# Low parts, squares and a norm's step move between GpSimd, adding DMAs and VectorE in a decoder trunk

## The chip, the cores and the metric

The kernel runs on one core of a Trainium2 chip. The metric is the device time of one execution in microseconds; the time before is the median of three runs. The engines are named as the profile names them: PE (TensorE matmuls), PEld (its weight loads), DVE (VectorE), ACT (ScalarE), POOL (GpSimd) and SP (SyncE, which here only issues DMAs). Each engine works through its own queue in order.

## The reference, cut to what matters

A decoder trunk of two layers, T = 512 rows, D = 1024. Layer 0 mixes tokens by differential attention with 8 heads, layer 1 by retention with 4 heads; behind each comes an MLP with a squared ReLU and a gated embedding.

```python
def sq_relu_mlp(xn, w1, w2):
    h = jax.nn.relu(xn @ w1)          # 1024 -> 4096
    return (h * h) @ w2               # 4096 -> 1024

def diff_attention(xn, ...):
    ...
    attn = a[:, :, 0] - lam * a[:, :, 1]
    o = attn @ v
    o = rms_norm(o, g_sub) * (1.0 - lambda_init)     # per head: the sub-norm
    return o @ w_o

def reference(x, p, ...):
    for i in range(2):
        h = rms_norm(x, norm_mix[i])
        x = x + (diff_attention(h, ...) if i % 2 == 0 else retention(h, ...))
        x = x + sq_relu_mlp(rms_norm(x, norm_mlp[i]), mlp_w1[i], mlp_w2[i])
        gate = jax.nn.sigmoid(rms_norm(x, norm_pe[i]) @ pe_w_gate[i])
        x = x + gate * (p[i] @ pe_w_up[i])
    return x
```

All is float32.

## The kernel before

Activations lie transposed, as 8 tiles of 128 features x 512 rows. Every factor of a matmul is kept as a pair: a high part (rounded to the matmul's format by a cast) and a low part (the value minus the high part). `mm3` (L262 to L266) forms one product as three matmuls, high x high (L264), high x low (L265) and low x high (L266).

**Weights.** The class `Weights` streams the weights in the order of their use, four pairs ahead of the one that PE reads. `load` fetches a 512 KB tile `raw` (three buffers, fetched by SP in program order), ACT casts it to `wh` (L101), and DVE writes `wl` = raw - wh (L105); there are five buffers each for `wh` and `wl`. While `W.by_dma` is set, the low part is made otherwise: ACT writes `wl` = -raw, rounded (L93), and POOL issues a DMA that adds `raw` onto `wl` in flight (L94). A raw buffer is free again when its last reader has finished, here that DMA. `by_dma` is set at the start of the attention (L408) and cleared in the MLP of layer 0, chunk 0, at hidden unit 4 (L754).

**The MLP.** It runs in four chunks of 1024 hidden features. In each chunk eight hidden units fill a PSUM tile `ph`; DVE drains it with the ReLU and the norm's factor into `ht` (L768), ACT squares it (L772), and `hh`, `hl` are split off by ACT (L241) and DVE (L242). The second matrix of the first three chunks (`MIXED`) goes by a Strassen scheme of seven products instead of eight. A chunk has two such rounds, r = 0 and r = 1. The scheme needs differences of the hidden blocks, `hu` (L786 to L788, split at L242), and sums and differences of the weight blocks, built by `Weights.mixed` on DVE: s1 = a21 + a22 (L129), s2 = s1 - a11 (L132), s4 = a12 - s2 (L136) and s3 = a11 - a21 (L139). The products run in the order a11, s1, s2, s4, s3, a12, a22. For each, ACT casts the high part (L146), and DVE subtracts it for the low part (L154), but for a11 and a22, where ACT writes the negative high part (L149) and POOL issues a DMA that fetches the block from HBM once more and adds it (L150).

`mix_round` (L710) accumulates the products in PSUM tiles called `py`, then layer, chunk, round, bank and half: py101b is layer 1, chunk 0, round 1, bank b, half 1. Bank b has three buffers, banks c and a two each. A finished part is added to the residual `x` by DVE (L729), and this frees the bank for the next round.

**The other places.** `squares` (L308) adds up squares of rows for a norm; ACT squares, and POOL adds (L314) unless another engine is given. In the attention each head ends in `values` (L562), which squares the head's PSUM tile `po` on ACT and splits the square into `osq...h` and `osq...l`, the low part on POOL, and in `sub_norm` (L575), whose steps go over ACT, DVE (L584), POOL (L585) and DVE (L586, which reads `po` last and frees its bank, and L587). The attention's units are set by a plan written by hand (`place`). At the end of the retention eight tiles `pus` of the last embedding are computed, copied from PSUM by ACT (L1030) and parked in HBM by DMAs from ACT's queue (L1031).

Apart from the hand plan and the DMAs kept in program order, the framework's scheduler sets the order of the instructions on each engine. It can put an instruction elsewhere when the work around it changes.

Of the kernel before, what the change touches and what calls it, by code (L numbers as in the profile page):

```python
# [13 lines left out]
ALU = mybir.AluOpType  # L14
AX = mybir.AxisListType

P = 128
# [47 lines left out]
class Weights:  # L65
# [42 lines left out]
    def mixed(self, kind, w, first):  # L108

        nc, mix = self.nc, self.mix  # L110
        i = len(self.made)
# [34 lines left out]
        nc.scalar.copy(out=hi, in_=t)  # L146
        if kind in ("a11", "a22"):

            nc.scalar.activation(out=lo, in_=hi.bitcast(F32), func=AF.Copy, scale=-1.0)  # L149
            nc.gpsimd.dma_start(  # L150
                out=lo.rearrange("p (j n) -> p j n", j=2), in_=source(0 if kind == "a11" else 3), accum_op=ALU.add
            )
        else:
            nc.vector.tensor_tensor(out=lo, in0=t, in1=hi.bitcast(F32), op=ALU.subtract)  # L154
# [13 lines left out]
def decoder_trunk(ctx: ExitStack, tc, xT, pT, small, dist, decay, ident,  # L168
# [200 lines left out]
    for k in range(KD):  # L369
        t = slot(f"xin{k}")  # L370
        load(t, xT[k])
        z.append(make_z(t, C_MIX, k))
        if k % 2 == 0:
            W.load()
            W.parts = 1
        squares(acc, t, k)

# [10 lines left out]
    with tc.tile_pool(name="at", bufs=1) as ap:  # L388
# [41 lines left out]
        gs = ap.tile([P, 1], F32, name="gs")  # L430
        nc.vector.tensor_scalar(out=gs, in0=sm[:, C_GSUB : C_GSUB + 1], scalar1=1.0 - LAM_INIT, scalar2=None, op0=ALU.mult)

# [129 lines left out]
        def values(h, kt):  # L562
# [7 lines left out]
            if kt == NT - 1:  # L570
                sq = slot("osq")
                nc.scalar.activation(out=sq, in_=po[h], func=AF.Square)
                po[h] = po[h], sq, slots(f"osq{h}", sq, lo_engine=nc.gpsimd)

        def sub_norm(h):  # L575
# [8 lines left out]
            nc.vector.scalar_tensor_tensor(out=u, in0=pn, scalar=P * EPS, in1=u, op0=ALU.add, op1=ALU.mult)  # L584
            nc.gpsimd.tensor_scalar(out=u, in0=u, scalar1=-0.5 / P, scalar2=1.5, op0=ALU.mult, op1=ALU.add)  # L585
            nc.vector.scalar_tensor_tensor(out=sq, in0=ps, scalar=gs, in1=sq, op0=ALU.mult, op1=ALU.mult)  # L586
            nc.vector.tensor_tensor(out=sq, in0=sq, in1=u, op=ALU.mult)  # L587
            oT[h] = slots(f"oT{h}", sq)
# [114 lines left out]
    def mlp(z, acc, layer, late_at=2):  # L703
# [43 lines left out]
        with tc.tile_pool(name=f"mlp{layer}", bufs=1) as mp:  # L747
            W.sums = mp
            for c in range(4):
# [3 lines left out]
                def begin(i):  # L753
                    if (layer, c, i) == (0, 0, 4):  # L754
                        W.by_dma = False
# [125 lines left out]
    with tc.tile_pool(name="zp", bufs=1) as zp:  # L881
# [9 lines left out]
        with tc.tile_pool(name="ret", bufs=1) as ap:  # L891
# [134 lines left out]
            for m in range(KD):  # L1026
# [3 lines left out]
                nc.scalar.copy(out=t, in_=pu)  # L1030
                nc.scalar.dma_start(out=up1[m // 2][:, m % 2, :], in_=t)  # L1031
            acc = project(RH - 1, go_before)
# [87 lines left out]
```

## Time and profile before

| | |
|---|---|
| Median of 3 runs | 1477.12 us (1475.58 to 1477.51) |
| Profiled execution, its own time | 1478.01 us |
| Its span in the trace | 1476.2 us |
| PE busy | 1444.1 us, 98% |
| DVE busy | 931.1 us, 63% |
| ACT busy | 728.0 us, 49% |
| POOL busy | 184.5 us, 12% |
| Mean granted clock of PE | 0.997 |

The execution is a little longer than its span in the trace, since some of it lies around the traced instructions. PE is the engine that is busy nearly all the time, so the list of its waits is short, and the other engines' timelines tell what each wait came from. A wait is put down to the instruction or DMA that came last; a DMA's time is that from its issue to its landing.

### The profile page before, as it was taken

The page shows a single profiled execution, that of the slowest core. Times are in us where ns is not written, and L with a number is a line of the kernel's source. Part 1 is how long each engine was busy: PE and PEld are TensorE (multiplying, and loading weights), DVE is VectorE, ACT ScalarE, POOL GpSimd, SP SyncE. Part 2 cuts the span into 40 slices and gives each one's busy share as a digit, 9 for nine tenths or more (in the row PEclk, how much of TensorE's full clock was granted, in tenths as well). Part 3 has the DMA queues.
Part 4 walks back from the last instruction along what each step waited for, and adds up shares of the span by engine and source line. Part 5 has one row for each costly group of instructions (what it writes and reads, how often), then busy time and mean ns, then how long its engine had stood idle before and what let it go on. Part 6 is the DMA issues. An engine that isn't in the chain of part 4 may idle for free.

```text
span 1476.2 us, 19408 instructions
## 1 busy us (share of the span) xinstructions
PE 1444.1 (98%) x7532; PEld 1224.4 (83%) x7532; DVE 931.1 (63%) x1465; ACT 728.0 (49%) x1091; POOL 184.5 (12%) x151
## 2 busy tenths in 40 slices
PE   9999989999999999999999999999999999999998
PEld 7777767889898988888888888888779889898887
DVE  6766777676676764486364555544698576675445
ACT  6777777754444444354442432433565354443432
POOL 4112112100000000211120210301230000000020
PEclk9999999999999999999999999999999999999999
DMA  6644566856355452243223232132334637445332
GB/s 227 143 115 114 129 168 142 216 143 184 104 136 151 113 165 93 63 165 122 79 83 105 65 112 93 58 128 72 129 100 113 173 86 186 114 121 152 98 114 86
DMA packets 65132, 183.14 MB, mean 124 GB/s; under 512 B 6033, under 2 KB 6545, under 8 KB 65041
## 3 DMA queue, kind: packets, MB, share of 16 engines
q1 hardware_dynamic: 51888, 147.31, 30.7%
q0 software_dynamic: 11424, 30.41, 12.0%
q10 hardware_dynamic: 1728, 4.20, 0.8%
q8 instruction: 59, 0.97, 0.3%
q14 instruction: 33, 0.26, 0.1%
HBM read 157.77 MB, written 6.29 MB: 111 GB/s over the span
## 4 chain that ended last, share of the span: by engine, by line
PE 77%; DMA 9%; DVE 5%; ACT 4%; issue 4%; POOL 1%; SPq 0%; DVEq 0%; POOLq 0%; ACTq 0%
PE ph L265 7%; PE ph L264 7%; PE ph L266 7%; DMA raw<-in_w 6%; PE pg L264 2%; PE pg L266 2%; PE pg L265 2%; PE rv L265 2%; PE py L265 2%; PE rqk L265 2%; PE rv L266 2%; PE rqk L266 2%; PE py L266 2%; PE py L264 2%; PE rv L264 2%
## 5 line engine op out<-in xcount | busy, mean ns | idle before, releaser
L101 ACT CAST wh<-raw 128x1024 fp32r<-128x1024 f32 (+1 forms) x163 | 170.2, 1046 | 345.2 <-PE ph L265 85.9
L105 DVE TENSOR_TENSOR wl<-raw,wh 128x1024 fp32r<-128x1024 f32 (+1 forms) x163 | 208.1, 1278 | 62.3 <-ACT wh L101 61.3
L265 PE MATMUL ph<-zl,wh 128*128 128x512 f32 x512 | 199.5, 390 | 0.0
L264 PE MATMUL ph<-zh,wh 128*128 128x512 f32 x512 | 199.3, 389 | 0.0
L266 PE MATMUL ph<-zh,wl 128*128 128x512 f32 x512 | 199.2, 389 | 0.0
L265 PEld LDWEIGHTS ph<-zl,wh 128*128 128x128 f32 x512 | 96.1, 188 | 20.6 <-DVE zl L245 0.8
L266 PEld LDWEIGHTS ph<-zh,wl 128*128 128x128 f32 x512 | 96.1, 188 | 19.9
L264 PEld LDWEIGHTS ph<-zh,wh 128*128 128x128 f32 x512 | 96.1, 188 | 19.8
L768 DVE SCALAR_TENSOR_TENSOR ht<-ph,rsm 128x512 f32<-128x512 f32 x64 | 43.9, 688 | 98.8 <-PE ph L266 98.6
L150 POOL DMA_DIRECT2D wl<-in_w x24 | 29.0, 1281 | 440.5 <-ACT wl L149 375.9
L146 ACT CAST wh<-mix 128x1024 fp32r<-128x1024 f32 x36 | 37.9, 1053 | 86.0 <-PE ph L265 23.3
L146 ACT CAST wh<-raw 128x1024 fp32r<-128x1024 f32 x48 | 49.2, 1049 | 56.3 <-PE ph L265 23.0
L265 PE MATMUL pqk<-wl,zh 128*128 128x512 f32 x128 | 51.1, 399 | 1.2 <-DMA wl<-raw 1.2
L264 PE MATMUL pqk<-wh,zh 128*128 128x512 f32 x128 | 51.6, 403 | 0.0
L264 PE MATMUL pg<-zh,wh 128*128 128x512 f32 (+1 forms) x136 | 51.2, 377 | 0.0
L266 PE MATMUL pg<-zh,wl 128*128 128x512 f32 (+1 forms) x136 | 51.2, 377 | 0.0
L265 PE MATMUL pg<-zl,wh 128*128 128x512 f32 (+1 forms) x136 | 51.2, 376 | 0.0
L266 PE MATMUL pqk<-wh,zl 128*128 128x512 f32 x128 | 51.0, 398 | 0.0
L264 PE MATMUL rg<-zh,wh 128*128 128x512 f32 x128 | 50.2, 392 | 0.0
L265 PE MATMUL rg<-zl,wh 128*128 128x512 f32 x128 | 50.1, 391 | 0.0
L266 PE MATMUL rg<-zh,wl 128*128 128x512 f32 x128 | 50.0, 390 | 0.0
L265 PE MATMUL rv<-wl,zh 128*128 128x512 f32 x128 | 49.8, 389 | 0.0
(1136 smaller groups left out, 4049.2 us busy)
## 6 DMA issues: line engine op xcount, KB each, us to landing
raw<-in_w SPq DMA_DIRECT2D x140, 512.0 KB, 3.8
wl<-raw POOLq DMA_DIRECT2D x34, 512.0 KB, 5.3
wl<-in_w POOLq DMA_DIRECT2D x24, 512.0 KB, 8.1
raw<-in_w_qk SPq DMA_DIRECT2D x16, 512.0 KB, 3.7
raw<-in_w_g SPq DMA_DIRECT2D x16, 512.0 KB, 3.8
raw<-in_w_rv SPq DMA_DIRECT2D x16, 512.0 KB, 3.6
raw<-in_w_rqk SPq DMA_DIRECT2D x16, 512.0 KB, 4.5
raw<-in_w_rg SPq DMA_DIRECT2D x16, 512.0 KB, 3.6
```

The source lines that it names most:

```text
L101: nc.scalar.copy(out=hi[:, s], in_=raw[:, s])
L105: e.tensor_tensor(out=lo[:, r], in0=raw[:, r], in1=hi[:, r].bitcast(F32), op=ALU.subtract)
L146: nc.scalar.copy(out=hi, in_=t)
L150: nc.gpsimd.dma_start(out=lo.rearrange("p (j n) -> p j n", j=2), in_=source(0 if kind == "a11" else 3), accum_op=ALU.add)
L264: nc.tensor.matmul(ps, a[0], b[0], start=start, stop=False, skip_group_check=on)
L265: nc.tensor.matmul(ps, a[0], b[1], start=False, stop=False, skip_group_check=on)
L266: nc.tensor.matmul(ps, a[1], b[0], start=False, stop=stop, skip_group_check=on)
L768: nc.vector.scalar_tensor_tensor(out=half, in0=s[1].rearrange("p (a n) -> p a n", a=2), scalar=0.0, in1=rs.rearrange("p (a n) -> p a n", a ...
```

## The change

Six edits, each of which takes work from POOL or from ACT's queue:

- `mixed`: only a22 gets its low part by an adding DMA; a11's is now made by DVE at L154. This concerns 12 products (2 layers, 3 chunks, 2 rounds).
- `by_dma` is cleared at hidden unit 0 in place of 4, so four more weights, the last of layer 0's first hidden units, get `wl` from DVE at L105.
- The first `squares` of the kernel: its seven adds go from POOL to DVE.
- `values`: the low parts of the eight heads' squares go from POOL to DVE.
- `sub_norm`: POOL's step goes. The constants are folded into `gs`, and two fused DVE operations take the place of POOL's and the two DVE operations behind it. The one that reads `po` is now the last.
- The eight DMAs of `pus` are issued by POOL in place of ACT.

```diff
--- before.py
+++ after.py
@@ -144,11 +144,11 @@
         hi = self.pool.tile([P, 1024], F32R, name=f"wh{i}", tag="wh", bufs=W_BUFS)
         lo = self.pool.tile([P, 1024], F32R, name=f"wl{i}", tag="wl", bufs=W_BUFS)
         nc.scalar.copy(out=hi, in_=t)
-        if kind in ("a11", "a22"):
+        if kind == "a22":
 
             nc.scalar.activation(out=lo, in_=hi.bitcast(F32), func=AF.Copy, scale=-1.0)
             nc.gpsimd.dma_start(
-                out=lo.rearrange("p (j n) -> p j n", j=2), in_=source(0 if kind == "a11" else 3), accum_op=ALU.add
+                out=lo.rearrange("p (j n) -> p j n", j=2), in_=source(3), accum_op=ALU.add
             )
         else:
             nc.vector.tensor_tensor(out=lo, in0=t, in1=hi.bitcast(F32), op=ALU.subtract)
@@ -373,7 +373,7 @@
         if k % 2 == 0:
             W.load()
             W.parts = 1
-        squares(acc, t, k)
+        squares(acc, t, k, nc.vector)
 
     def up_unit(pu, wu, p, m):
         for j in range(2):
@@ -428,7 +428,7 @@
         nc.vector.tensor_scalar(out=gq, in0=sm[:, C_GQ : C_GQ + 1], scalar1=-(DH ** -0.5), scalar2=None, op0=ALU.mult)
         gk = sm[:, C_GK : C_GK + 1]
         gs = ap.tile([P, 1], F32, name="gs")
-        nc.vector.tensor_scalar(out=gs, in0=sm[:, C_GSUB : C_GSUB + 1], scalar1=1.0 - LAM_INIT, scalar2=None, op0=ALU.mult)
+        nc.vector.tensor_scalar(out=gs, in0=sm[:, C_GSUB : C_GSUB + 1], scalar1=-(1.0 - LAM_INIT) / (2.0 * P), scalar2=None, op0=ALU.mult)
 
         for tt in range(NT):
             put_v(pv[tt], 0, tt)
@@ -570,7 +570,7 @@
             if kt == NT - 1:
                 sq = slot("osq")
                 nc.scalar.activation(out=sq, in_=po[h], func=AF.Square)
-                po[h] = po[h], sq, slots(f"osq{h}", sq, lo_engine=nc.gpsimd)
+                po[h] = po[h], sq, slots(f"osq{h}", sq)
 
         def sub_norm(h):
             ps, sq, pair = po.pop(h)
@@ -582,9 +582,8 @@
             u = slot("osu")
             nc.scalar.activation(out=u, in_=sq, func=AF.Square)
             nc.vector.scalar_tensor_tensor(out=u, in0=pn, scalar=P * EPS, in1=u, op0=ALU.add, op1=ALU.mult)
-            nc.gpsimd.tensor_scalar(out=u, in0=u, scalar1=-0.5 / P, scalar2=1.5, op0=ALU.mult, op1=ALU.add)
-            nc.vector.scalar_tensor_tensor(out=sq, in0=ps, scalar=gs, in1=sq, op0=ALU.mult, op1=ALU.mult)
-            nc.vector.tensor_tensor(out=sq, in0=sq, in1=u, op=ALU.mult)
+            nc.vector.scalar_tensor_tensor(out=u, in0=u, scalar=-3.0 * P, in1=sq, op0=ALU.add, op1=ALU.mult)
+            nc.vector.scalar_tensor_tensor(out=sq, in0=ps, scalar=gs, in1=u, op0=ALU.mult, op1=ALU.mult)
             oT[h] = slots(f"oT{h}", sq)
 
 
@@ -751,7 +750,7 @@
                 hs, st = [], {}
 
                 def begin(i):
-                    if (layer, c, i) == (0, 0, 4):
+                    if (layer, c, i) == (0, 0, 0):
                         W.by_dma = False
                     return W.next(), ps_mm(f"ph{layer}{c}{i}")
 
@@ -1028,7 +1027,7 @@
                 up_unit(pu, wu, p1, m)
                 t = zslot(f"pus{m}", F32)
                 nc.scalar.copy(out=t, in_=pu)
-                nc.scalar.dma_start(out=up1[m // 2][:, m % 2, :], in_=t)
+                nc.gpsimd.dma_start(out=up1[m // 2][:, m % 2, :], in_=t)
             acc = project(RH - 1, go_before)
             z = zn
 
```

The matmuls are the same, 7517 in the program. POOL has 156 instructions before and 125 after, ACT 1041 and 1017, DVE 1467 and 1498. Behind L584 the lines after are one lower than before, so L729 is L728, L768 is L767, and L786 is L785. Three places show what stands in a row.

DVE at the start of the second round in layer 1, chunk 1, before (numbers behind a name tell buffers apart; py110b and py110c are banks of round 0, L129 and L132 build s1 and s2, and raw_0 is a11):

```order
L729 TENSOR_TENSOR x_2463<-x_2463,py110c_10583 128x256
L729 TENSOR_TENSOR x_2269<-x_2269,py110b_10541 128x256
L729 TENSOR_TENSOR x_2404<-x_2404,py110b_10555 128x256
L729 TENSOR_TENSOR x_2269<-x_2269,py110c_10573 128x256
L729 TENSOR_TENSOR x_2404<-x_2404,py110c_10583 128x256
L129 TENSOR_TENSOR mix_10671<-raw_2_10667,raw_3_10669 128x1024
L729 TENSOR_TENSOR x_2319<-x_2319,py110b_10541 128x256
L132 TENSOR_TENSOR mix_10703<-mix_10671,raw_0_10634 128x1024
L154 TENSOR_TENSOR wl_10674<-mix_10671,wh_10673 128x1024
L729 TENSOR_TENSOR x_2463<-x_2463,py110b_10555 128x256
```

And after:

```order
L728 TENSOR_TENSOR x_2458<-x_2458,py110c_10562 128x256
L728 TENSOR_TENSOR x_2265<-x_2265,py110b_10520 128x256
L728 TENSOR_TENSOR x_2399<-x_2399,py110b_10534 128x256
L154 TENSOR_TENSOR wl_10616<-raw_0_10613,wh_10615 128x1024
L728 TENSOR_TENSOR x_2265<-x_2265,py110c_10552 128x256
L728 TENSOR_TENSOR x_2399<-x_2399,py110c_10562 128x256
L129 TENSOR_TENSOR mix_10649<-raw_2_10645,raw_3_10647 128x1024
L728 TENSOR_TENSOR x_2314<-x_2314,py110b_10520 128x256
L132 TENSOR_TENSOR mix_10681<-mix_10649,raw_0_10613 128x1024
L154 TENSOR_TENSOR wl_10652<-mix_10649,wh_10651 128x1024
L728 TENSOR_TENSOR x_2458<-x_2458,py110b_10534 128x256
```

After, the split of a11 (`wl` from raw_0) stands among the drains of round 0, ahead of L129; the rest of the order is the same.

DVE in the MLP of layer 0, chunk 0, behind the norm (`ph` is a hidden unit's PSUM tile), before:

```order
L318 RECIPROCAL rsm_3003<-rsm_3003 128x512
L768 SCALAR_TENSOR_TENSOR ht<-ph_3014,rsm_3003 128x512
L768 SCALAR_TENSOR_TENSOR ht<-ph_3022,rsm_3003 128x512
L768 SCALAR_TENSOR_TENSOR ht<-ph_3104,rsm_3003 128x512
L786 TENSOR_TENSOR hu<-ht 128x512
L242 TENSOR_TENSOR hl<-ht,hh 128x256
L242 TENSOR_TENSOR hl<-ht,hh 128x512
L787 TENSOR_TENSOR hu<-ht,hu 128x256
L788 TENSOR_TENSOR hu<-ht,hu 128x256
L768 SCALAR_TENSOR_TENSOR ht<-ph_3143,rsm_3003 128x512
L242 TENSOR_TENSOR hl<-hu,hh 128x1024
L242 TENSOR_TENSOR hl<-ht,hh 128x256
```

And after:

```order
L318 RECIPROCAL rsm_2995<-rsm_2995 128x512
L767 SCALAR_TENSOR_TENSOR ht<-ph_3005,rsm_2995 128x512
L105 TENSOR_TENSOR wl_3001<-raw_2999,wh_3000 128x1024
L767 SCALAR_TENSOR_TENSOR ht<-ph_3012,rsm_2995 128x512
L105 TENSOR_TENSOR wl_3008<-raw_3006,wh_3007 128x1024
L242 TENSOR_TENSOR hl<-ht,hh 128x256
L785 TENSOR_TENSOR hu<-ht 128x512
L105 TENSOR_TENSOR wl_3089<-raw_3087,wh_3088 128x1024
L242 TENSOR_TENSOR hl<-ht,hh 128x512
L786 TENSOR_TENSOR hu<-ht,hu 128x256
L767 SCALAR_TENSOR_TENSOR ht<-ph_3093,rsm_2995 128x512
L787 TENSOR_TENSOR hu<-ht,hu 128x256
```

After, the splits at L105 are interleaved with the hidden units' drains and their splits.

ACT at the end of the retention, where the `pus` tiles are copied among the last heads' casts (`goh`) and weight casts, before:

```order
L241 CAST goh<-ro 128x512
L1030 COPY pus_9148<-pu_9141 128x512
L1031 DMA up_182<-pus_9148 128x512
L241 CAST goh<-ro 128x512
L1030 COPY pus_9158<-pu_9151 128x512
L1030 COPY pus_9168<-pu_9161 128x512
L1031 DMA up_182<-pus_9158 128x512
L101 CAST wh_9136<-raw_9135 128x1024
L1031 DMA up_182<-pus_9168 128x512
```

And after:

```order
L241 CAST goh<-ro 128x512
L1029 COPY pus_9130<-pu_9123 128x512
L1029 COPY pus_9140<-pu_9133 128x512
L241 CAST goh<-ro 128x512
L1029 COPY pus_9150<-pu_9143 128x512
L101 CAST wh_9118<-raw_9117 128x1024
L1029 COPY pus_9160<-pu_9153 128x512
L1029 COPY pus_9170<-pu_9163 128x512
L1029 COPY pus_9180<-pu_9173 128x512
```

After, the DMAs are no longer in ACT's queue, and the second copy stands ahead of the `goh` cast that it stood behind.

## Rows read from the trace of the kernel before

**Rows 1.** The page, busy time of each engine, its share and instructions.

```profile
PE 1444.1 (98%) x7532; PEld 1224.4 (83%) x7532; DVE 931.1 (63%) x1465; ACT 728.0 (49%) x1091; POOL 184.5 (12%) x151
```

**Rows 2.** Waits of PE: tile, line <- releaser: total us, times, longest.

```profile
PE py000b L265 <- DVE hl L242: 1.8, 1, 1.8
PE py101b L266 <- DMA wl<-in_w: 1.8, 2, 1.3
...
PE py021b L266 <- DMA wl<-in_w: 1.4, 1, 1.4
...
PE ptqk L480 <- DVE qkt L464: 1.4, 2, 0.9
...
PE py121b L266 <- DMA wl<-in_w: 1.2, 2, 0.8
...
PE py000b L266 <- DMA wl<-in_w: 1.0, 1, 1.0
...
PE py011b L266 <- DMA wl<-in_w: 1.0, 1, 1.0
...
PE py111b L266 <- DMA wl<-in_w: 0.8, 1, 0.8
PE pu L264 <- ACT pus L1030: 0.7, 1, 0.7
PE pn L323 <- POOL osq2l L242: 0.6, 1, 0.6
...
PE py001b L264 <- DVE x L729: 0.5, 1, 0.5
...
PE py001b L266 <- DMA wl<-in_w: 0.5, 1, 0.5
PE py000b L264 <- ACT hh L241: 0.4, 1, 0.4
PE py111b L264 <- DVE x L729: 0.3, 1, 0.3
```

**Rows 3.** Windows: stretch, us, busy by engine, granted clock (0.50), DMA share, GB/s.

```profile
324.30:327.70 3.40, 3.40 (x18) 3.40 (x17) 3.40 (x7) 2.21 (x3) 0.00 (x0) 0.50 0.28 71
```

**Rows 4.** Timeline, DVE, layer 0, chunk 0: start, us, instruction [idle before <- releaser].

```profile
311.40 1.23 DVE L129 TENSOR_TENSOR mix<-raw,raw 128x1024 f32<-128x1024 f32 x1 [5.62 <-DMA raw<-in_w]
312.54 0.68 DVE L768 SCALAR_TENSOR_TENSOR ht<-ph,rsm 128x512 f32<-128x512 f32 x1
```

**Rows 5.** Timeline, DVE, start of the second round in layer 1, chunk 1.

```profile
1233.49 1.23 DVE L136 TENSOR_TENSOR mix<-raw,mix 128x1024 f32<-128x1024 f32 x1 [2.41 <-DMA raw<-in_w]
1234.63 0.41 DVE L729 TENSOR_TENSOR x<-x,py110b 128x256 f32<-128x256 f32 x1
```

**Rows 6.** The page, DMA issues of the whole span: count, KB, median us to landing.

```profile
raw<-in_w SPq DMA_DIRECT2D x140, 512.0 KB, 3.8
```

**Rows 7.** DMAs issued from 1107.0 to 1107.9 us: one adding, one fetch.

```profile
wl<-in_w POOLq DMA_DIRECT2D x1, 512.0 KB, 6.4
raw<-in_w SPq DMA_DIRECT2D x1, 512.0 KB, 6.0
```

**Rows 8.** DMAs issued from 1138.5 to 1139.5 us, second round, layer 1, chunk 0.

```profile
wl<-in_w POOLq DMA_DIRECT2D x1, 512.0 KB, 9.6
raw<-in_w SPq DMA_DIRECT2D x1, 512.0 KB, 8.3
```

**Rows 9.** The page, costliest groups: count | busy us, mean ns | idle before.

```profile
L150 POOL DMA_DIRECT2D wl<-in_w x24 | 29.0, 1281 | 440.5 <-ACT wl L149 375.9
```

**Rows 10.** Timeline, ACT, end of the retention.

```profile
1052.41 0.62 ACT L241 CAST goh<-ro 128x512 fp32r<-128x512 f32 x1 [2.37 <-POOL ro L1009]
```

**Rows 11.** Timeline, all engines, attention, from 203.9 to 205.3 us.

```profile
203.95 1.29 POOL L242 TENSOR_TENSOR osq4l<-osq,osq4h 128x512 fp32r<-128x512 f32 x1 [7.28 <-ACT osq4h L241]
204.10 1.16 DVE L457 TENSOR_TENSOR qkr<-qku,qky 128x8 f32<-128x8 f32 x1
```

**Rows 12.** Timeline, DVE, hidden units of layer 1, chunk 1.

```profile
1212.17 0.69 DVE L768 SCALAR_TENSOR_TENSOR ht<-ph,rsm 128x512 f32<-128x512 f32 x1 [2.29 <-PE ph L266]
```

## The prediction

> **What bounds the kernel now.** I read the page first: TensorE (PE) is busy 1444.1 us, 98% of the span, and VectorE (DVE), ScalarE (ACT) and GpSimd (POOL) are far below it [rows 1]. The change leaves every matmul in place, so it can win only time in which PE stands still or runs slowly. The second view is therefore the list of what PE waited for; its rows that touch an edit are [rows 2]. They fall into four places.
>
> (a) The first round of chunk 0 in layer 0's MLP: 0.4 us for `hh`, 1.8 us for `hl`, and directly behind them 3.4 us at a granted clock of 0.50, the 1.2 GHz level, before it is 1.00 again [rows 3].
>
> (b) The start of every second round (tiles py001b, py011b, py021b, py101b, py111b, py121b, so six places): PE waits first for a11's low part, whose adding DMA has not landed, 0.5 + 1.0 + 1.4 + 1.3 + 0.8 + 0.8 = 5.8 us (of the two-wait rows the longest is meant), and then for a drain `x` at L729 that clears the bank, 0.5 us once and 0.3 us at five places, 2.0 us together [rows 2].
>
> (c) One 0.7 us wait for `pus`. (d) In the attention 0.9 us (the longest of `ptqk`'s two) and 0.6 us for `osq2l` [rows 2].
>
> The third view is DVE's timeline, for why (a) and (b) happen. At (a) DVE stands at L129 for 5.62 us until a raw fetch lands; the L768 drain of `ht` is queued behind it, so the hidden units come late [rows 4]. At (b) DVE stands at L136 for 2.41 us until the a12 fetch lands, with the bank's drain behind it [rows 5].
>
> The fourth view is the flight of single DMAs. The usual raw fetch takes 3.8 us [rows 6]. Issued beside one adding DMA it took 6.0 us [rows 7]; at a start like (b), where the a22 and the a11 adding DMAs both fly, the a12 fetch took 8.3 us and the adding DMA 9.6 us [rows 8]. So one cause feeds both waits at (b): the a11 add is late itself, and slows the fetch that blocks DVE.
>
> **The change part by part.** The sum is made against the profiled execution, 1478.0 us, 0.9 us above the median of the runs, 1477.1.
>
> *a11 without the adding DMA.* Twelve times an ACT pass, a POOL issue (1281 ns mean, [rows 9]) and a 512 KB transfer go; twelve times a DVE split is added. A DVE operation of two 128x1024 inputs takes 1.23 us [rows 4, 5]: 14.8 us more on an engine that is idle over a third of the span. The split needs only the raw tile, which was fetched before too, and the ACT cast. At a second round the order puts it between bank drains, ahead of L129. So the 5.8 us go; what takes their place is the split's 1.23 us, at a point where DVE's next drains wait for PE anyway. The 2.0 us of drain wait go only if the a12 fetch lands earlier by what PE now arrives earlier: 0.5 + 0.5 us at the least, 1.4 + 0.3 = 1.7 us at the most. A flight of 8.3 us that becomes 6.0 us gives 2.3 us, and one that becomes 3.8 us gives 4.5 [rows 6 to 8]. Where PE now arrives latest the margin is thin, so I take 7.5 of the 7.8 us; bounds: 0 (the wait only moves to the drain) and 7.8.
>
> *The last four weights of layer 0's first MLP part, and a11, by DVE.* L94's adding DMAs hold a raw buffer until they land. That is why the fetch that L129 needs is issued late and then flies beside adds. Now DVE frees the buffer. Five splits, 5 x 1.23 = 6.2 us, come ahead of the hidden drains, and the 5.62 us of standing at L129 [rows 4] should shrink to little, with DVE idle time from other drains on top. Layer 1 makes the same weights on DVE already, and no wait for `hl` or `hh` at its place is in [rows 2]'s list (0.2 us and more). So (a) should go: 0.4 + 1.8 + half of 3.4 = 3.9 us. Lower bound of the gain: 0.4 us, if the splits make `hl` just as late and the slow stretch stays. I take 3.9.
>
> *a22 at layer 0, chunk 0, first round* (1.0 us for py000b's `wl`, [rows 2]). It keeps its adding DMA, but the a11 add that stands ahead of it on POOL's queue and the late fetches are gone. Bounds 0 and 1.0; I take 0.9, since layer 1's same product has no such row in the list.
>
> *pus DMAs from ACT's queue to POOL's.* ACT stood 2.37 us at a `goh` cast that needed POOL's `ro`, with the next `pus` copy behind it [rows 10]. The order now has that copy ahead of the cast: 0.7 us go [rows 2]. The eight DMAs are issued by POOL; the nearest row, an adding issue, is 1281 ns [rows 9], so about 10 us on an engine that is 12% busy [rows 1], behind its `ro` multiplications. What is queued behind them there is only the next norm's sums. If that cover were gone, up to 10 us would delay that norm. I take -0.7, bounds -0.7 and 0.
>
> *Attention.* The eight low parts of the heads' squares and the sub-norm's step go to DVE; the step disappears as an instruction of its own, because two fused operations take the place of three. Two things are better: the 0.6 us for `osq2l`, and the small DVE operations beside a POOL one, such as the 1.16 us for a 128x8 operation during POOL's 1.29 us [rows 11], behind which `ptqk` waited 0.9 us. One is worse: DVE gets eight operations of 128x512, of the size of L768's 0.68 us [rows 4], and the operation that reads `po`, and so frees its bank, comes after the other two. Gain at most 1.5 us; loss at most 8 x 0.68 = 5.4 us if every head pays. PE's waits name two heads of eight, so the ends are near each other in effect, and I take 0.
>
> *Squares of the first rows.* Seven adds go to DVE, 7 x 0.68 = 4.8 us. PE's list has no wait for a `zl` of that stretch. If DVE were late, 4.8 us would be the most. I take 0.
>
> Sum: 3.9 + 7.5 + 0.9 + 0.7 = 13.0, so 1478.0 - 13.0 = 1465.0 us.
>
> **The rivals.**
>
> *1. The wait only moves* at the six second rounds: a11's low part is in time, but PE comes 1 us earlier to a bank whose drain still waits behind L136. For it: the drain wait stands directly behind the DMA wait at all six, and if a fetch's flight did not depend on what flies beside it, PE's gain at the low part would be lost at the drain to the last tenth. Against it: the flights, 8.3 us beside two adds, 6.0 us beside one, 3.8 us as a rule [rows 6 to 8]. It gives 1465.0 + 7.5 = 1472.5 us. The Trainium skill, "DMA: Bandwidth & Descriptors", section "Anatomy of one DMA", gives a transfer on GpSimd's path as 2.0 us plus its bytes over 436 GB/s, by which I estimate 3.2 us for 512 KB, with no term for what flies beside it. By that rule removing an add speeds up nothing else, and the outcome is this rival, 1472.5 us. The trace disagrees: the adds took 6.4 and 9.6 us [rows 7, 8].
>
> *2. The attention pays.* If half of the heads pay the full operation, 4 x 0.68 = 2.7 us, the time is 1467.7 us. For it: DVE is the busiest helper there, and the bank is freed last. Against it: [rows 2] show waits at few heads.
>
> *3. Slower: DVE late for each first round.* The split of a11 is put into the run of hidden drains. At layer 1, chunk 1, DVE is idle for 2.29 us before the round's last drain [rows 12], which takes the 1.23 us. If the cast comes late instead, the split is taken after that idle time and pushes `hl` at the start of five first rounds by 1.23 us, 6.2 us together, and in chunk 0 the five splits add their 6.2 us to the 1.8 us wait, while (a) stays. Less (b)'s 7.5, 0.9 and 0.7 us, this is 12.4 - 9.1 = +3.3, so 1481.3 us. It decides from the point where the idle time before the last drain is under 1.23 us. Against it: the 2.29 us, and layer 1, whose DVE does the weight splits already.
>
> **How the numbers follow.** Forecast 1465.0 us (its small misses in the attention included): 0.70. Rival 1: 0.13. Rival 2: 0.10. Rival 3: 0.04. The remaining 0.03 is a mixture in which (a) and (b) both stay and the rest cancels, about 1477. A measurement of this kernel tells some 0.2%, 3 us, from no change. Faster by more than that are the forecast, rivals 1 and 2, less a tail in which rival 1 comes with the attention's loss: 0.90. Within: 0.06. Slower: 0.04. The low end takes everything at its best, 7.8 + 3.9 + 1.0 + 0.7 + 1.5 = 14.9 us off the median 1477.1, with 1 us of play for smaller waits: 1461. The high end is rival 1 with 1.5 us of attention loss, 1474.
>
> **What would show it.** Right: no wait of PE for `wl<-in_w` at the six second rounds, nor a 0.3 us one for `x` behind it; DVE's stand at L136 under 1 us; a12 flights of 6 us or less; PE at full clock through 324 to 328 us; no wait for `pus`. PE's idle time at these places should be 11.3 us less, and 1.7 us come from the clock. Wrong: a wait for `x` of 1 us or more at py011b; a wait for `hl` at py010b, py110b and the like; waits for `po` or `pn` in the attention that are new; a late `rsm1` after the pus DMAs.

## The result and the profile after

The kernel after takes 1454.74 us (median of 4 runs, 1452.58 to 1455.94), the kernel before 1476.35 us in the same comparison. The ratio is 0.9852, with an interval from 0.9835 to 0.9869: 21.8 us less, between 19.3 and 24.4. The forecast was 1465.0 us, its range 1461 to 1474. The direction and the main places were right. The size was not: the time lies below the range.

The page of the kernel after, busy time of each engine (to be read beside [rows 1]):

```profile
PE 1435.0 (99%) x7532; PEld 1219.9 (84%) x7532; DVE 949.5 (65%) x1496; ACT 712.6 (49%) x1075; POOL 142.8 (10%) x120
```

What PE waited for in the kernel after (tile, line <- releaser: total us, times, longest; to be read beside [rows 2]):

```profile
PE ps L508 <- DVE kl L245: 1.7, 2, 1.5
PE po L264 <- ACT aT0h L241: 1.4, 1, 1.4
PE pt L559 <- DVE aT0l L242: 1.2, 1, 1.2
...
PE py001b L266 <- DMA wl<-in_w: 0.5, 1, 0.5
```

Of the fourteen rows in [rows 2], py001b's is the only one of the MLP that is left (it is another instance, in the last product of that round), and one of `ptqk` stays with 0.5 us. The waits for `hl`, for a11's `wl`, for the drain `x`, for `pus` and for `osq2l` are gone. The slow stretch in the first round of layer 0's MLP is gone too. Before, the stretch of [rows 3] began 5.2 us into the round, at a granted clock of 0.50. Here are two windows that cover nearly all of the round in the kernel after (stretch, us, busy time by engine, then the granted clock, 1.00, DMA share, GB/s):

```profile
314.10:317.50 3.40, 3.40 (x30) 3.40 (x30) 3.36 (x7) 2.20 (x4) 0.00 (x0) 1.00 0.71 210
317.50:333.00 15.50, 15.50 (x132) 15.50 (x131) 12.21 (x20) 6.12 (x6) 1.22 (x1) 1.00 0.57 156
```

DVE at the start of the second round in layer 1, chunk 1, kernel after (timeline; start, us, instruction, in brackets idle time before it):

```profile
1201.60 1.23 DVE L154 TENSOR_TENSOR wl<-raw,wh 128x1024 fp32r<-128x1024 f32 x1 [0.77 <-ACT wh L146]
1202.74 0.97 DVE L728 TENSOR_TENSOR x<-x,py110c 128x256 f32<-128x256 f32 x2
1205.05 1.23 DVE L129 TENSOR_TENSOR mix<-raw,raw 128x1024 f32<-128x1024 f32 x1 [1.34 <-DMA raw<-in_w]
...
1210.93 1.22 DVE L136 TENSOR_TENSOR mix<-raw,mix 128x1024 f32<-128x1024 f32 x1
```

The first row is a11's split, in idle time, as the order had it. The last is L136, before which DVE no longer stands idle for the a12 fetch (2.41 us in [rows 5]). That fetch, in the DMAs issued from 1206 to 1207 us of the kernel after, took 3.7 us:

```profile
raw<-in_w SPq DMA_DIRECT2D x1, 512.0 KB, 3.7
```

**Where the time went.** The table takes the start of the first matmul of each stage in the two traces, and for the last row the end of the last matmul.

| Stage (from the first matmul of ... to that of ...) | Before, us | After, us | Less |
|---|---|---|---|
| span's start to the attention's first `ps` | 45.67 | 43.33 | 2.34 |
| `ps` to layer 0's first hidden unit | 229.38 | 225.73 | 3.65 |
| py000 to py001 (first round, chunk 0) | 25.69 | 20.15 | 5.54 |
| py001 to py010 | 65.17 | 64.41 | 0.76 |
| py011 to py020 | 65.67 | 63.71 | 1.96 |
| py021 to the retention's first `rqk` | 176.64 | 174.41 | 2.23 |
| first `pu` of the pus tiles to layer 1's first hidden unit | 33.97 | 33.00 | 0.97 |
| py100 to py101 | 20.53 | 20.15 | 0.38 |
| py101 to py110 | 66.51 | 63.71 | 2.80 |
| py111 to py120 | 65.52 | 63.71 | 1.81 |
| py121 to the end | 153.92 | 151.72 | 2.20 |
| all others | 523.04 | 523.28 | -0.24 |
| sum | 1471.71 | 1447.31 | 24.40 |

The two profiled executions lie 24.4 us apart in their matmuls, the medians 21.6. The difference is spread from run to run, and the experiments show where most of the change sits. The six stages that begin with a second round gave 11.8 us, where the prediction had 7.5. They add up to 570.3 us in the kernel before, and to 571.6 to 574.7 us in the profiles of the four experiments below that leave the second rounds alone (the last four weights, the attention, the squares and `pus`). So this profile of the kernel before shows the least that was lost there.

**Why more than the listed idle time.** The timeline of PE in the kernel before, around one such wait (start, us, instruction, idle before it):

```profile
1232.12 0.28 PE L264 MATMUL py111b<-hh,wh 128*128 128x256 f32 x1
1232.24 0.28 PE L265 MATMUL py111b<-hl,wh 128*128 128x256 f32 x1
1233.33 0.36 PE L266 MATMUL py111b<-hh,wl 128*128 128x256 f32 x1 [0.81 <-DMA wl<-in_w]
1233.53 0.28 PE L264 MATMUL py111b<-hh,wh 128*128 128x256 f32 x1
1233.65 0.28 PE L265 MATMUL py111b<-hl,wh 128*128 128x256 f32 x1
```

In these rows matmuls overlap: undisturbed, one starts 0.12 us behind the other, though by the profile each lasts 0.28. Across the wait the starts are 1.09 us apart, 0.97 more than 0.12, though the listed idle time is 0.81. The next start comes after 0.20 in place of 0.12. The wait cost 1.05 us, 0.24 more than the list says. Read in the same way, the other thirteen waits of the six second-round stages in the kernel before cost 0.23 to 0.26 us each on top of their idle time; the fourteen come to 12.2 us, 8.8 listed and 3.4 for the restarts. The Trainium skill, "TensorE: Matmul & The Clock Gate", section "Single matmul latency", gives a single bf16 matmul at 2.4 GHz 398 cycles on top of its columns, 0.27 us for 256 columns by that estimate. The rows agree, 0.28 us. The list counts idle time only from the end of those 0.28 us, though undisturbed the next matmul starts after 0.12: that is the 0.16 us between 0.97 and 0.81. The 0.08 us of the start behind it come on top.

### The profile page after: what moved, and what is told of

Read it like the earlier page. It is cut to its first block, busy times and chain, and to the rows that moved or that the text cites. A ratio compares the mean times of both kernels' runs of the same rounds, so it can differ in the third digit from the quotient of the medians.

```text
span 1451.9 us, 19320 instructions
## 1 busy us (share of the span) xinstructions
PE 1435.0 (99%) x7532; PEld 1219.9 (84%) x7532; DVE 949.5 (65%) x1496; ACT 712.6 (49%) x1075; POOL 142.8 (10%) x120
## 4 chain that ended last, share of the span: by engine, by line
PE 89%; DVE 3%; ACT 3%; DMA 3%; issue 1%; POOL 0%; SPq 0%; ACTq 0%; DVEq 0%; POOLq 0%
PE ph L265 8%; PE ph L264 8%; PE ph L266 8%; PE rg L264 2%; PE rg L265 2%; PE pg L266 2%; PE rg L266 2%; PE pg L264 2%; PE pg L265 2%; PE rv L264 2%; PE py L264 2%; PE rqk L266 2%; PE rqk L264 2%; PE rv L266 2%; PE py L265 2%; PE rv L265 2%
## 5 line engine op out<-in xcount | busy, mean ns | idle before, releaser
L101 ACT CAST wh<-raw 128x1024 fp32r<-128x1024 f32 (+1 forms) x167 | 174.3, 1045 | 344.7 <-PE ph L265 85.8
L105 DVE TENSOR_TENSOR wl<-raw,wh 128x1024 fp32r<-128x1024 f32 (+1 forms) x167 | 211.2, 1266 | 54.7 <-ACT wh L101 53.6
L767 DVE SCALAR_TENSOR_TENSOR ht<-ph,rsm 128x512 f32<-128x512 f32 x64 | 44.0, 689 | 93.9 <-PE ph L266 93.6
L146 ACT CAST wh<-mix 128x1024 fp32r<-128x1024 f32 x36 | 37.9, 1052 | 62.2 <-DVE mix L136 21.6
L150 POOL DMA_DIRECT2D wl<-in_w x12 | 14.4, 1201 | 461.7 <-DVE wl L154 365.2
L264 PE MATMUL rx<-goh,wh 128*128 128x512 f32 x128 | 49.8, 389 | 0.0
```

Source lines behind the costliest of these rows:

```text
L101: nc.scalar.copy(out=hi[:, s], in_=raw[:, s])
L105: e.tensor_tensor(out=lo[:, r], in0=raw[:, r], in1=hi[:, r].bitcast(F32), op=ALU.subtract)
L150: nc.gpsimd.dma_start(out=lo.rearrange("p (j n) -> p j n", j=2), in_=source(3), accum_op=ALU.add)
L264: nc.tensor.matmul(ps, a[0], b[0], start=start, stop=False, skip_group_check=on)
L767: nc.vector.scalar_tensor_tensor(out=half, in0=s[1].rearrange("p (a n) -> p a n", a=2), scalar=0.0, in1=rs.rearrange("p (a n) -> p a n", a ...
```

## The experiments

The first four kernels are the kernel before with one part of the change each.

**a11's low part by DVE, alone.**

```diff
-        if kind in ("a11", "a22"):
+        if kind == "a22":
...
-                out=lo.rearrange("p (j n) -> p j n", j=2), in_=source(0 if kind == "a11" else 3), accum_op=ALU.add
+                out=lo.rearrange("p (j n) -> p j n", j=2), in_=source(3), accum_op=ALU.add
```

> The kernel before with one edit: a11's low part by DVE. Theory 1 (an avoided wait of PE gives its idle time and about 0.2 us of restart on top): the twelve waits at the six second rounds, 7.8 us of idle time by the list, give 10.2 us, as the two traces lie apart there; 1466 us, and the a12 fetch flies 6 us or less. Theory 2 (a wait gives its idle time alone, as the prediction had it): 7.5 us, 1469 us. Theory 3 (the wait only moves to the drain): under 2 us, 1475 us. The first 262 us are as before: what they show is the spread of the start and of the stretch around 91 us from run to run.

Measured: 1459.02 us against 1478.17, ratio 0.9876 (0.9857 to 0.9895), 18.3 us less. By stages the six second-round stages give 12.4 us, the first round of chunk 0 goes from 25.69 to 22.05 us, and py100 to py101 gives 0.4. Together 16.4 us come from the MLP. The other 2 us are within the interval. All waits at the second rounds are gone, and so is the wait for `hl` at py000b; the a22 wait there stays, 0.9 us, and a wait of 0.4 us for a drain is new there. The six a12 flights at second rounds are 3.8 to 4.8 us. So theory 1 has the mechanism right, and theories 2 and 3 fall. Its 1466 us was 7 us too many: the second rounds gave 12.4 us in place of 10.2, and the first round of chunk 0 was left out. This one edit is most of the change.

**The last four weights by DVE, alone.**

```diff
-                    if (layer, c, i) == (0, 0, 4):
+                    if (layer, c, i) == (0, 0, 0):
```

> The kernel before with one edit: the last four weights of layer 0's first hidden units by DVE. Theory 1 (their adding DMAs alone hold the raw buffers, so hl is late and the clock falls): 3.9 to 4.3 us less, 1472 us, no half clock near 324 us. Theory 2 (a11's add is as much to blame): the wait for hl shrinks to some 1 us and the slow stretch may stay, 1 to 2 us less, 1475 us. The first 262 us are as before.

Measured: 1472.52 us, ratio 0.996 (0.9945 to 0.9974), 5.9 us less. py000 to py001 takes 20.15 us, the full 5.5 us of that stage, with no `hl` wait and no half clock there. The second rounds keep theirs. This is theory 1, with 1.2 us more than the most it foresaw for that stage. With a11's edit 3.6 us of the same 5.5 had come. The wait for `hl` goes with either edit, the a22 wait behind it with this one; the two must not be added.

**The attention's two edits, alone.**

```diff
...
-                po[h] = po[h], sq, slots(f"osq{h}", sq, lo_engine=nc.gpsimd)
+                po[h] = po[h], sq, slots(f"osq{h}", sq)
...
-            nc.gpsimd.tensor_scalar(out=u, in0=u, scalar1=-0.5 / P, scalar2=1.5, op0=ALU.mult, op1=ALU.add)
-            nc.vector.scalar_tensor_tensor(out=sq, in0=ps, scalar=gs, in1=sq, op0=ALU.mult, op1=ALU.mult)
-            nc.vector.tensor_tensor(out=sq, in0=sq, in1=u, op=ALU.mult)
+            nc.vector.scalar_tensor_tensor(out=u, in0=u, scalar=-3.0 * P, in1=sq, op0=ALU.add, op1=ALU.mult)
+            nc.vector.scalar_tensor_tensor(out=sq, in0=ps, scalar=gs, in1=u, op0=ALU.mult, op1=ALU.mult)
```

The cut leaves out the changed constant in `gs`.

> The kernel before with two edits: the low parts of the heads' squares and the sub-norm's step on DVE. Theory 1 (the stretch around 91 us belongs to the change of the start, or to chance): 1.3 us less, from the waits at 137, 206 and 229 us, 1475 us, and the wait of 2.6 us for kl with the half clock at 92 us stays. Theory 2 (the stretch around 91 us belongs to this edit): 4 us less, 1472.5 us, and that wait is 1.5 us at full clock. Prediction's rival 2: slower by 2.7 us.

Measured: 1478.28 us, ratio 1.0006 (0.9992 to 1.0021), which is anything from 1.2 us less to 3.1 us more. Neither theory's gain shows; the 2.7 us of the prediction's rival 2 are not excluded by the time. What PE waited for there:

```profile
PE pt L559 <- DVE aT0l L242: 1.2, 1, 1.2
...
PE ptqk L480 <- DVE qkt L464: 0.5, 1, 0.5
...
PE pt L559 <- DVE osu L584: 0.3, 1, 0.3
PE po__2471 L264 <- DVE x L637: 0.3, 1, 0.3
```

`osq2l` and the 0.9 us of `ptqk` are gone as foreseen, 1.5 us together. But the wait for `aT0l`, 0.5 us in the kernel before, is 1.2 us, and the last two rows are new, 1.3 us together, so in this list gains and losses nearly cancel. The longer wait for `aT0l` is no loss of DVE's, though. The transposes `pt` around it, in the kernel before and then here:

```profile
225.11 0.44 PE L559 MATMUL pt<-idn,e 128*128 128x128 f32 x2 [0.20 <-DVE e L550]
...
226.97 0.55 PE L559 MATMUL pt<-idn,e 128*128 128x128 f32 x3 [0.50 <-DVE aT0l L242]
```

```profile
222.24 0.44 PE L559 MATMUL pt<-idn,e 128*128 128x128 f32 x2
...
224.10 0.55 PE L559 MATMUL pt<-idn,e 128*128 128x128 f32 x3 [1.19 <-DVE aT0l L242]
```

They stand 1.86 us apart in both, and in both DVE stands idle for 0.56 us until ACT's `aT0h` is there. PE has four other matmuls between them before and one here, so it only waits longer for the same thing.

**The squares of the first rows by DVE, alone.**

```diff
-        squares(acc, t, k)
+        squares(acc, t, k, nc.vector)
```

> The kernel before with one edit: the seven adds of the first squares on DVE. Theory 1 (POOL's adds held up DVE, and PE starts and rises to full clock earlier): 2.3 us less by 10 us into the span, as in the trace after, or up to 4.6 us if the stretch around 91 us follows; 1472 to 1474 us. Theory 2 (the start's 2.3 us are the spread of DMA landings from run to run): within 1 us of before, and the first raw part's landing, 6.0 us before and 4.9 us after, varies with no link to the edit.

Measured: 1473.82 us, ratio 0.9979 (0.9967 to 0.9991), 3.1 us less, between 1.3 and 4.9. This was expected at zero in the prediction. The stretch from the first `pv` to the first `ps` takes 37.30 us, against 38.98 in the kernel before. Two things go with the length of that stretch, and the table below of all traces tells them apart: when PE's clock rises to 2.4 GHz, and which engine adds the squares. In the kernel before, the matmuls of 128x512 start 0.42 us apart until the rise at 10.3 us and 0.22 us apart behind it (PE; start, us, instruction):

```profile
9.42 0.63 PE L265 MATMUL pv<-wl,zh 128*128 128x512 f32 x1
9.84 0.60 PE L266 MATMUL pv<-wh,zl 128*128 128x512 f32 x1
...
10.52 0.39 PE L266 MATMUL pv<-wh,zl 128*128 128x512 f32 x1
10.74 0.40 PE L265 MATMUL pv<-wl,zh 128*128 128x512 f32 x1
```

The granted clock that the windows print is 1.00 there too, so the rise is read from the matmuls. It varies between executions whose first instructions are the same, and comes early and late with either engine, so theory 1's reason, an earlier rise by the edit, does not hold. Theory 2's "within 1 us" falls by the time.

| Clock full from | Squares on POOL: first `pv` to first `ps`, us | Squares on DVE, us |
|---|---|---|
| 9.5 us or later | 38.96, 38.98, 39.14 | 38.96, 39.11 |
| 3.9 to 6.6 us | 38.26, 38.35, 38.49, 39.09, 39.47 | 37.30, 37.72, 37.72 |

With the late clock the stretch takes 38.96 to 39.14 us with either engine. With the early one PE waits for DVE, whose operations are stretched while POOL adds. DVE in the kernel after with the squares given back to POOL (timeline; it is the eighth experiment):

```profile
10.48 1.32 DVE L245 SCALAR_TENSOR_TENSOR zl<-xin,sm,zh 128x512 fp32r<-128x512 f32 x1 [0.39 <-ACT zh L244]
11.94 2.09 DVE L105 TENSOR_TENSOR wl<-raw,wh 128x1024 fp32r<-128x1024 f32 x1
```

and in the kernel after:

```profile
12.86 0.75 DVE L245 SCALAR_TENSOR_TENSOR zl<-xin,sm,zh 128x512 fp32r<-128x512 f32 x1
13.52 0.69 DVE L314 TENSOR_TENSOR acc_a<-acc_a,sq 128x512 f32<-128x512 f32 x1
14.12 1.22 DVE L105 TENSOR_TENSOR wl<-raw,wh 128x1024 fp32r<-128x1024 f32 x1
```

What PE waits for in the first of these two kernels:

```profile
PE pv L265 <- DVE wl L105: 0.8, 1, 0.8
```

Such a row, of 0.4 to 0.8 us, stands in all five profiles with an early clock and the squares on POOL, and in none of the other eight. The profile of the kernel before had its clock rise at 10.3 us, so this wait was not in its list. By the table the edit is worth 0.5 to 2.2 us where the clock rises early; what is left of the 3.1 us isn't settled.

The next two ask why the second rounds waited.

**a11's transfer kept, with no reader.** The split goes to DVE, but ACT's negative copy and the adding DMA stay, into a tile that nobody reads.

```diff
+        if kind == "a11":
+            idle = self.sums.tile([P, 1024], F32R, name=f"idle{i}", tag="idle", bufs=1)
+            nc.scalar.activation(out=idle, in_=hi.bitcast(F32), func=AF.Copy, scale=-1.0)
+            nc.gpsimd.dma_start(out=idle.rearrange("p (j n) -> p j n", j=2), in_=source(0), accum_op=ALU.add)
-        if kind in ("a11", "a22"):
+        if kind == "a22":
...
```

> The edit of a11 alone (low part by DVE), but ACT's negative copy and the adding DMA stay, into a tile of their own that nobody reads: the company of the transfer without its lateness. Theory 1 (the adds' company makes the a12 fetch slow, so DVE stands at L136 and PE waits for the drain): the wait for the low part is gone, the one for x grows to what PE comes earlier, the a12 flight stays at 7 to 8.3 us, and less than half of the 12.4 us that the second rounds gave in the kernel with that edit alone is left: 1470 us or more. Theory 2 (lateness alone; the fetch is slow for another reason or its slowness does not matter): as the edit alone, 1459 us.

Measured: 1479.15 us, ratio 1.0003 (0.9987 to 1.0018). All of the 18 us is gone again. Waits of PE in this kernel (its lines are four higher, so L733 is L729, the drain):

```profile
PE py021b L268 <- DVE x L733: 1.8, 1, 1.8
PE py000b L269 <- DVE hl L246: 1.8, 1, 1.8
PE py011b L268 <- DVE x L733: 1.5, 1, 1.5
...
PE py111b L268 <- DVE x L733: 1.4, 1, 1.4
PE py101b L268 <- DVE x L733: 1.3, 1, 1.3
...
PE py121b L268 <- DVE x L733: 1.2, 1, 1.2
...
PE py001b L268 <- DVE x L733: 1.2, 1, 1.2
```

No second round waits for a11's low part any more (the rows for `wl` that are left, up to 0.7 us, belong to a22), and the drain waits have grown from 2.0 to 8.4 us. DMAs issued from 1131.6 to 1134.2 us, at one of these starts:

```profile
wl<-in_w POOLq DMA_DIRECT2D x1, 512.0 KB, 6.2
idle<-in_w POOLq DMA_DIRECT2D x1, 512.0 KB, 9.4
raw<-in_w SPq DMA_DIRECT2D x1, 512.0 KB, 8.0
```

And DVE, which waits for that fetch with the drain behind it:

```profile
1142.07 1.23 DVE L136 TENSOR_TENSOR mix<-raw,mix 128x1024 f32<-128x1024 f32 x1 [3.34 <-DMA raw<-in_w]
1143.21 0.41 DVE L733 TENSOR_TENSOR x<-x,py100b 128x256 f32<-128x256 f32 x1
```

In this kernel the six a12 fetches of the second rounds are issued 5.5 to 6.9 us before the round and fly 6.8 to 8.0 us; with a11's edit alone they are issued 5.1 to 6.4 us before it and fly 3.8 to 4.8 us. So the transfer's company is the cause, not its lateness alone: theory 1. This is what the prediction's rival 1 describes.

**a22 by DVE, a11 by the adding DMA.**

```diff
-        if kind in ("a11", "a22"):
+        if kind == "a11":
...
```

> The mirror of the change: a22's low part by DVE, a11 keeps the adding DMA. Theory 1 (two adds at once are the trouble at the second rounds, either may go): a11's add then lands some 3 us earlier (6.4 us for 9.6 us) and the a12 flight is 6 us or less; the second rounds lose their waits and 12 us go there, but chunk 0 of layer 0 keeps part of its waits: 1463 us. Theory 2 (a11's add is late by its place): waits for wl of 0.5 to 1.4 us stay at the second rounds, 1472 us.

Measured: 1462.23 us, ratio 0.9885 (0.9866 to 0.9905), 17 us less. The six second-round stages lose their waits but for one of 0.1 us. At py101, the add issued at 1127.5 us lands after 7.3 us, and the a12 fetch issued at 1131.6 us after 4.5, where both were 9.6 and 8.3 in [rows 8]. The `hl` wait of 1.8 us at py000b stays, as in the kernel just above. This is theory 1: it was two adds at once, and either could go.

The a12 fetches of all rounds of four kernels (the three with an edit of a11 or a22 and the one with the last four weights) sort by their company:

| Adds in flight with it | Flight of the 512 KB fetch, us |
|---|---|
| none | 3.5 to 3.8 |
| one | 3.5 to 6.1 |
| two, issued 1.6 to 3.4 us before it | 6.8 to 8.0 |

**The pus DMAs from POOL, alone.**

```diff
-                nc.scalar.dma_start(out=up1[m // 2][:, m % 2, :], in_=t)
+                nc.gpsimd.dma_start(out=up1[m // 2][:, m % 2, :], in_=t)
```

> The kernel before with one edit: the eight DMAs of pus from POOL's queue. Theory 1: the 0.7 us wait of PE goes and with it a restart, 1.0 us less in the stretch of the pus tiles (33.0 us in place of 34.0), which the time can hardly tell: 1477 us. Theory 2 (POOL's issues delay the sums behind them): a new wait at the norm of layer 1's MLP, 1 us or more, slower by that.

Measured: 1476.05 us against 1477.87, ratio 0.9992 (0.9977 to 1.0007). The stretch takes 33.00 us in place of 33.97: 1.0 us, the idle 0.7 and a restart, as theory 1 had it; the whole time cannot tell it. Nothing new waits at the next norm.

The last four runs are the kernel after, whole or less one part.

**The squares back on POOL.** The edit of the fourth kernel taken out of the kernel after.

> The kernel after with one edit taken back: the first seven adds of squares on POOL again. Theory 1 (that edit is worth what it seemed alone, 3 us): 1457.5 us. Theory 2 (its 3 us were the spread of the start and of the attention): within 1 us of the kernel after, 1454.7 us; the stretch from the first pv to the first ps takes 37 us where the clock is full early and 39 us where it isn't, whatever the squares do.

Measured: 1459.18 us, ratio 0.9864 (0.9842 to 0.9886). Theory 2 falls by the table above, in which its profile is the 39.47 us with an early clock. By the ratios this kernel is 1.8 us slower than the next, and their intervals overlap. Its profile also has waits for a22's adding DMA, 0.8 us at py000b and 0.5 us at py100b, which the next one's has not, and these two stages are 1.8 us longer. So the edit's worth here isn't decided.

**The kernel after once more, without any adding DMA in the Strassen rounds, and without the attention's edits.** These three ran beside each other. The second one's edit to the kernel after:

```diff
-        if kind == "a22":
+        if kind == "none":
...
```

> The kernel after, once more, to stand beside the two runs next to it: 1454.7 us by its first times. The stretch from the first pv to the first ps 37.2 to 37.8 us, the second rounds without waits but for 0.5 us at chunk 0.

> The kernel after, with a22's low part by DVE too: no adding DMA is left in the Strassen rounds. Theory 1 (one add alone does no harm, nor any good): the 0.5 us wait at chunk 0 and its restart go, 0.7 us, and DVE takes the twelve splits in its idle time; 1454 us, not to be told from the kernel after. Theory 2 (DVE has become tight in the rounds): new waits for hl or x, 0.2 to 1 us at each of twelve rounds, 1457 to 1466 us.

> The kernel after with the attention's two edits taken back (heads' low parts and the sub-norm's step on POOL again). Theory 1 (their gains and losses cancel, as in the kernel with these edits alone): 1454.7 us, within 1.5 us. Theory 2 (they help once the rest is clean): 1457 us or more.

Measured: 1456.21 us, ratio 0.9852 (0.9833 to 0.987); 1456.13 us, 0.9859 (0.9841 to 0.9877); 1458.04 us, 0.9872 (0.9853 to 0.989). The kernel after has a late clock in this profile and takes 38.96 us from the first `pv` to the first `ps`, not the 37.2 to 37.8 that were expected. Without the last adds the 0.5 us wait at py001b is gone and no new one above 0.1 us appears in the MLP, but the time is not to be told from the kernel after: theory 1, and DVE has room for twelve more splits.

The kernel without the attention's edits is slower than the kernel after, by 1.8 us in the medians and 3.0 by the ratios, whose intervals overlap. That is the time of theory 2, but its trace does not show theory 2's reason. What PE waits for in its MLP, whose instructions are those of the kernel after, in the same order on each engine:

```profile
PE py021b L266 <- DMA wl<-in_w: 1.5, 1, 1.5
...
PE py001b L266 <- DMA wl<-in_w: 1.1, 1, 1.1
...
PE py100b L266 <- DMA wl<-in_w: 0.4, 1, 0.4
```

All three are a22's adding DMA, now the only one. In the two second rounds it took 9.1 and 9.8 us beside the fetches of the weights behind it. These stages are 3.2 us longer than in the second profile of the kernel after, more than the 2.1 us that lie between the ends of the two traces, while the attention, from its first `ps` to layer 0's first hidden unit, is 1.2 us shorter. So what the attention's edits are worth is not shown, and one add alone is not always harmless: in four profiles of the same MLP its waits are 0.2, 0.5, 1.3 and 2.9 us. None of the kernels is clearly faster than the one after.

The traces show why the attention is so hard to judge. From its first `ps` to layer 0's first hidden unit the eight profiles without its edits take 224.9 to 231.6 us, the five with them 225.7 to 228.1. All instructions up to layer 0's first hidden unit are the same in the kernel before and in five of the experiments (a11 alone, the last four weights alone, a11's transfer kept, a22 by DVE, pus alone); they reach it at 275.0, 270.6, 271.5, 269.1, 273.3 and 276.0 us. The kernel after gets there at 269.1 us, and in its second profile at 272.3. Part of the spread is the clock. Windows of the second profile of the kernel after, two stretches in the attention:

```profile
183.62:187.02 3.40, 3.40 (x8) 2.73 (x9) 3.05 (x17) 2.20 (x6) 0.00 (x0) 0.50 0.99 227
224.58:227.98 3.40, 3.40 (x10) 2.58 (x9) 1.71 (x4) 0.80 (x1) 0.85 (x1) 0.50 0.30 57
```

PE before each of them:

```profile
183.54 0.76 PE L264 MATMUL po<-aT0h,v100h 128*128 128x512 f32 x1 [1.44 <-ACT aT0h L241]
```

```profile
222.66 0.55 PE L559 MATMUL pt<-idn,e 128*128 128x128 f32 x3 [1.19 <-DVE aT0l L242]
224.02 0.50 PE L264 MATMUL po__2563<-oT0h,wh 128*128 128x512 f32 x1 [0.82 <-DVE x L637]
```

Each stretch follows waits of over a microsecond and costs at most 1.7 us, half its length, and the same waits stand in other profiles without it. The second stretch shows in three of the five profiles with the attention's edits and in none of the eight without (the kernel before among them). The edits may bring it on; no run shows that they do.

## Why the prediction was wrong in size

**The step that failed** is the pricing of PE's waits: the sum took the idle time of the list. It stands in the prediction's first part, "0.5 + 1.0 + 1.4 + 1.3 + 0.8 + 0.8 = 5.8 us" and "2.0 us together". From start to start each wait costs 0.23 to 0.26 us more. At the second rounds the restarts of the twelve waits that were counted are 2.9 us. The same step left out the second wait of py101b and py121b, which the list gives as one of two; they are a22's in the second round, 0.4 us of idle time each, 1.3 us with their restarts, and they went too. In (a), with a22's wait in the same round, 4.8 us were taken and 5.5 came. For `pus` 0.7 were taken and 1.0 came.

**The second rounds (term of 7.5 us).** Mechanism right, size wrong: 11.8 us in the kernel after, 12.4 us by a11's edit alone. That one cause feeds both waits was shown: with the transfer kept, the gain is nil. The margin that was called thin was wide enough: in the kernel after the six flights are 3.7 to 5.7 us, and at py021b, where PE had waited longest, 4.5.

**The four weights and a11 (3.9 us).** Right in mechanism. Not seen was that either edit alone frees `hl`; the experiments showed 5.5 and 3.6 us of the same 5.5.

**a22 at chunk 0 (0.9 us).** Right for the kernel after, where py000b has no wait left. The four weights' edit took it away, a11's left 0.9 us of it. In part this is luck: in the kernel with the squares back on POOL, whose MLP is the same, it was 0.8 us again.

**The attention (0).** Not contradicted: 1.0006, with an interval of 1.2 us less to 3.1 more. The loss that was priced, at the operation that frees `po`, has no row. What stands against the 1.5 us in the list is mainly `aT0l`, which comes no later than before while PE comes earlier. So the zero is in part luck.

**The squares (0).** Wrong: alone the edit gave 3.1 us, at least 1.3. The argument was that PE's list had no wait there; but that list came from an execution whose clock was at half speed until 10.3 us, and the wait shows only where it rose earlier.

**The rivals.** Rival 1 did not come, and the kernel with the transfer kept shows what it looks like. In the Trainium skill, "DMA: Bandwidth & Descriptors", section "Anatomy of one DMA", the fit for a transfer on GpSimd's path has no term for its company. The traces disagree: of two adds at once the first took 5.5 to 6.9 us and the second 8.9 us or more, and the fetch, which SP issues, 3.5 to 3.8 us alone and 6.8 us or more beside both. Rival 2, the attention's loss, has no row at the operation that frees `po`; the only row of the sub-norm is the 0.3 us for `osu`. Rival 3, late `hl` at the first rounds, has no row either: all six first rounds of the kernel after take 20.15 us.

**The range.** Its low end was "everything at its best", 14.9 us, with 1 us of play. The stages behind the attention alone gave 18.4 us (5.54 + 11.76 + 0.97 + 0.38 - 0.24, table above) where the sum had 13.0. From 1478.0 that is 1459.6 us, already below the low end: an error in the price of each wait goes through every term, and the bounds had been worked out with the same price. The other 3.4 us of the 21.8 stay open. In the two traces all that is left, 6.0 us, lies in the first 275 us, with the squares among it. But that part spreads by 6.9 us between executions of the same instructions, and the second rounds took up to 4.4 us more in other profiles with the same code than in the one that was read.

## What to carry to other kernels

Price a wait of PE from the start of the matmul ahead of it to that of the second one behind it, not by the idle time that a list gives; many short waits are worth far more than their sum. Before a transfer is called late, count what flies beside it: here a fetch beside one adding DMA came in time, and beside two it took twice as long and blocked an in-order engine with a drain behind it. The one adding DMA that is left still came up to 1.5 us late in some profiles. A profile is one execution, so a wait can be missing from it because the clock was low, and a stage's gain should be held against the spread of the same stage in kernels that leave it alone.

## What the hardware showed that was not expected

- A 512 KB fetch took 3.5 to 3.8 us alone and 6.8 to 8.3 us beside two adding DMAs of the same size, which themselves took 5.5 to 6.9 us (the first) and 8.9 to 9.7 us (the second). Once, at py101 of the kernel with the pus DMAs alone, it was 9.6 us for the fetch and 11.2 for the second add.
- One adding DMA of 512 KB from HBM, with no other add in flight, took 5.4 to 9.8 us, often beside several fetches.
- In the kernel before a wait of PE between matmuls of 128x256 at full clock cost 0.23 to 0.26 us on top of its idle time.
- The clock rose to 2.4 GHz at 3.9 to 10.3 us into the span in executions whose first instructions are the same, and fell to 1.2 GHz for stretches of 3.4 us behind waits in some executions and not in others.
- DVE operations took 1.3 and 2.1 us in place of 0.75 and 1.22 while POOL added tiles of 128x512.
